# Holding the dense products of an RWKV-7 stage together on the tensor engine

## The chip, the core and the metric

The kernel runs on one core of a Trainium2 chip. The core has a tensor engine (PE, whose weight loads the profile lists as PEld), a vector engine (DVE), a scalar engine (ACT), a general engine (POOL) and a queue that issues transfers (SP). Each engine takes its instructions in the order in which the program lists them. The metric is the device time of one execution in microseconds, lower is better.

## The reference

The computation is a small decoder trunk in float32: 256 tokens of width 2048, one RWKV-7 layer, one latent-attention layer, each followed by a squared-ReLU MLP. The change is in the RWKV layer alone. Cut to what matters there:

```python
rkv = jnp.einsum('jbtd,jde->jbte', xs[:3], w_rkv)      # three 2048x2048 projections
r, k, v = rkv[0], rkv[1], rkv[2]
decay = jnp.exp(-jnp.exp(w_log))                       # w_log from tanh(xw @ w1) @ w2
a = jax.nn.sigmoid(a0 + (xa @ a1) @ a2)
g = jax.nn.sigmoid(xg @ g1) @ g2

def step(S, inp):                                      # a recurrence over 256 tokens, per head of 64
    sa = jnp.einsum('bhvk,bhk->bhv', S, -kk_t)
    S = (S * w_t[:, :, None, :] + sa[..., None] * (kk_t * a_t)[:, :, None, :]
         + v_t[..., None] * k_t[:, :, None, :])
    return S, jnp.einsum('bhvk,bhk->bhv', S, r_t)

_, y = lax.scan(step, S0, ...)
out = (group_norm(y) + bonus) * g
return out @ w_o                                       # one more 2048x2048 projection
```

## The kernel before

**Precision.** A large product is made of three products in a rounded 32-bit type (fp32r). Each operand is split into a high part (a cast on ACT, line 172) and a low part (a subtraction on DVE, line 173). For a weight they are called `whi` and `wlo`, and one half of a loaded weight block (`raw`) is 128x1024. Both come from a pool with two buffers each, and the small weights `wsm` of a tile use the same two.

**The RWKV stage.** The 2048 channels are done in 16 tiles of 128 channels (two heads). For each tile `project_rk` makes r and k: two weights of two halves each, 8 blocks a half, 3 products a block, so 96 products of 128x256 (`rk`, lines 223 to 225). These are the dense filling. `rwkv_tile` does the rest of the tile as a long chain of small steps with a `yield` after each: the small projections `wa` (decay and a) and `pg` (gate), 6 products each; matrices within the chunk (`pm`, `ar`); a triangular inverse by doubling (`pW`, `pN`, `pW`, `pN`, `pT`, `pW`, `pN`, tiles of 32 then 64, in fp32); the recurrence over two chunks (`pu`, `psS`, `prhs`, `py`); and a group norm (`yt`). Almost every step of that chain goes from PE to ACT or DVE and back to PE.

**The loop.** Up to three tiles are under way (`LONG`), each begun 9 rounds (`STAGGER`) after the one before. A round advances each of them by one step and then takes from the dense filling: in the kernel before, 16/9 of a `yield` a round, and a `yield` stands after every second block (6 products). When the last tile has begun, the filling is the output projection of the first 12 of 16 channel blocks (`out_start`, `pos`, 288 products of 128x512), 2.5 blocks a round, each block of 3 products followed by a `yield`. After the loop `proj_tail` adds the last four channel blocks (`po`), with the rows of the gate (`grow`) made on PE.

**What sets the order.** A scheduler places each engine's instructions: the order of the text gives priorities, and among what it holds to be ready the first in priority goes first. So small products stand between any two dense products where the scheduler expects them ready. One helper of the kernel fixes an order: `together` gives its first product to the scheduler and puts the others, at high priority, right behind it:

```python
    def together(*calls):
        ins = calls[0]().ins
        with tc.issue_after(ins), tc.high_priority():
            for c_ in calls[1:]:
                c_()
```

Before the change it is used for the small products of one step only (`pm`, `pW`, `pN`, `psS`).

Beside this, `pump` puts steps of another computation (conditioning columns, DVE line 320, `raw` from `in_adat_dram`) behind each weight half, at a set rate.

Of the kernel before, what the change touches and what calls it, by code (L numbers as in the profile page):

```python
# [20 lines left out]
P = 128  # L21
D = 2048
KT = D // P
T = 256
# [9 lines left out]
STAGGER = 9  # L34
# [3 lines left out]
PACE = 2.5  # L38
# [38 lines left out]
def trunk_kernel(ctx: ExitStack, tc: tile.TileContext, a, out, dbg=None):  # L77
# [65 lines left out]
    def product(*args, **kw):  # L143
        return lambda: PE.matmul(*args, **kw)

# [242 lines left out]
    with ExitStack() as s0:  # L388
# [162 lines left out]
        with ExitStack() as s2:  # L551
# [24 lines left out]
            def project_rk(i):  # L576

                ps = banks["rk"].tile([P, 512], F32, tag="rk", name="rk")
                res = []
                for w, name in enumerate(("wr", "wk")):  # L580
                    raw = load(a[name][i])
                    o = slice(w * T, (w + 1) * T)
                    for half in range(2):
                        hi = split["hi"].tile([P, 1024], F32R, tag="whi", name="whi")
                        lo = split["lo"].tile([P, 1024], F32R, tag="wlo", name="wlo")
                        hilo(hi, lo, raw[:, half * 1024 : half * 1024 + 1024])
                        pump(rate[0])
                        for j in range(8):
                            kt = half * 8 + j
                            s = slice(j * P, (j + 1) * P)  # L590
                            mm3w(ps[:, o], hi[:, s], lo[:, s], xs_at(w, 0, kt), xs_at(w, 1, kt), kt == 0, kt == KT - 1)
                            if j % 2:
                                yield
                    res.append(tmp("rk"[w] + "S"))
                    ACT.copy(res[w], ps[:, o])  # L595
                rks[i] = res

            def rwkv_tile(i):
# [9 lines left out]
                yield  # L608
                wa = tbank("wa", "rb")
                for z, (zh, zl) in enumerate(((zw_h, zw_l), (za_h, za_l))):  # L610
                    q = slice(z * P, (z + 1) * P)
                    mm3w(wa[:, z * T : (z + 1) * T], smh[:K1, q], sml[:K1, q], zh[:K1], zl[:K1], True, True)
# [116 lines left out]
                for j in range(15):  # L729
# [4 lines left out]
                    if j == 4:  # L734
                        (smh, sml), = unit(a["wsm"][i][:, T:], T)
                        yield
                    if j == 9:
                        pg_ = tbank("pg", "rb")
                        for g in range(2):
                            s = slice(g * P, (g + 1) * P)  # L740
                            mm3w(pg_[:, :T], smh[:, s], sml[:, s], sg_h[:, g, :], sg_l[:, g, :], g == 0, g == 1)
# [145 lines left out]
            def out_start():  # L887

                for i in range(KO):
                    split_o(i)  # L890
                    yield
                for n in range(4):
                    pss = [banks[k].tile([P, 512], F32, tag=k, name="pos") for k in ("rk", "mm")]
                    for g in range(KO // 4):
                        for half, (hi, lo) in enumerate(unit(a["wo"][n, g])):
                            for j in range(2):
                                kt = g * 4 + half * 2 + j
                                s = slice(j * 512, (j + 1) * 512)
                                for t in range(2):
                                    q = slice(t * P, (t + 1) * P)  # L900
                                    mm3(pss[t], o_h[:, kt, q], o_l[:, kt, q], hi[:, s], lo[:, s], kt == 0, kt == KO - 1)
                                    yield
# [6 lines left out]
            for _ in project_rk(0):  # L909
                pass  # L910
            flying, nxt, steps = [], 0, 0
            fill, owed, pace = iter(()), 0.0, 16 / STAGGER
            while nxt < KT or flying:
                if nxt < KT and len(flying) < LONG and steps >= STAGGER * nxt:
                    for _ in fill:
                        pass
                    flying.append(rwkv_tile(nxt))
                    nxt += 1
                    if nxt < KT:
                        fill = project_rk(nxt)  # L920
                    else:
# [4 lines left out]
                        fill, pace = out_start(), PACE  # L926
                        rate[0] = RATE_T
                steps += 1
                for g_ in list(flying):
                    if next(g_, 0) == 0:  # L930
                        flying.remove(g_)

                owed += pace if flying else 48
                while owed >= 1:
                    owed -= 1
                    next(fill, 0)
            for _ in fill:
                pass
# [633 lines left out]
```

## Time and profile before

| | |
|---|---|
| median of 3 runs | 2593.98 us (2587.92 to 2596.9) |
| the profiled execution | 2599.04 us |
| its span, first to last instruction | 2597.3 us |
| RWKV stage, first `rk` product to last `pos` product | from 218.7 to 779.7 us |
| PE busy over the span | 2487.8 us (96%) |
| DVE busy over the span | 1945.7 us (75%) |

Times in the text are microseconds from the start of the span. In a row of the timeline the first number is the start, the second the time from start to end; products overlap, so the distance from one start to the next is what a product costs the engine, and the busy time is not. "[0.93 <-DVE rst L159]" says that the engine stood idle for 0.93 us, and what ended it. A row with xN stands for N entries in one go; a product in plain fp32 (not fp32r) makes two entries. "PEclk" is the clock that the tensor engine was granted, as a share of full speed.

### The profile page before, as it was taken

Reading aid. Unit: us, or ns where it says so; the run is one execution under the profiler, and the core shown is the slowest. Engines: PE = TensorE matmul, PEld = TensorE weight load, DVE = VectorE, ACT = ScalarE, POOL = GpSimd, SP = SyncE. Lnnn points to the kernel's source line nnn. Section 1 sums busy time; section 2 is a strip of 40 time slices with the busy share of each in tenths; the row PEclk is TensorE's granted clock in tenths of the full one; section 3 lists DMA queues with packets and bytes.
Section 4 is the critical chain, followed back from the end, with each engine's and each line's share of the span. In section 5 each row is a group of like instructions: output and inputs, shape, how many; then the busy total and the mean of one; then the engine's idle time right before and its main releaser. Section 6 shows DMA issues by size and latency. Waiting matters only on the chain.

```text
span 2597.3 us, 39264 instructions
## 1 busy us (share of the span) xinstructions
PE 2487.8 (96%) x15048; PEld 2060.5 (79%) x15048; DVE 1945.7 (75%) x3823; ACT 1312.5 (51%) x2361; POOL 70.9 (3%) x150
## 2 busy tenths in 40 slices
PE   6998999999997999999999999999899999999998
PEld 3667887888776888888888878778788888888886
DVE  4787887888877788888888867776676665555555
ACT  3555675766646444444444456544544444444443
POOL 0000110111100000000000000000000000000000
PEclk8899998999998999999999999999999999999999
DMA  9755544455575688888888824657567555555553
GB/s 374 293 192 196 178 173 153 166 180 186 171 265 205 227 331 327 331 322 328 327 332 332 328 103 156 217 176 254 210 223 260 186 190 195 189 185 194 192 184 127
DMA packets 87885, 594.54 MB, mean 229 GB/s; under 512 B 10128, under 2 KB 14480, under 8 KB 16784
## 3 DMA queue, kind: packets, MB, share of 16 engines
q1 hardware_dynamic: 87696, 592.03, 63.0%
q8 instruction: 118, 1.93, 0.3%
q14 instruction: 71, 0.58, 0.1%
HBM read 589.89 MB, written 2.10 MB: 228 GB/s over the span
## 4 chain that ended last, share of the span: by engine, by line
PE 77%; DVE 8%; ACT 4%; issue 1%; DMA 1%; POOL 0%; DVEq 0%; ACTq 0%
PE pup L233 17%; PE pd L218 9%; PE pd L220 9%; PE pd L219 9%; PE pup L234 9%; DVE wlo L173 2%; DVE raw L320 1%; PE po L219 1%; PE po L220 1%; PE po L218 1%; PE rk L223 1%; PE rk L224 1%; PE rk L225 1%; PE pl L218 1%; PE ar L720 1%
## 5 line engine op out<-in xcount | busy, mean ns | idle before, releaser
L172 ACT CAST whi<-raw 128x1024 fp32r<-128x1024 f32 x729 | 743.9, 1023 | 895.1 <-PE pd L220 355.9
L173 DVE TENSOR_TENSOR wlo<-raw,whi 128x1024 fp32r<-128x1024 f32 x729 | 864.0, 1188 | 439.0 <-ACT whi L172 436.1
L233 PE MATMUL pup<-h,whi 128*128 128x512 f32 x1920 | 677.8, 398 | 0.0
L234 PE MATMUL pup<-h,wlo 128*128 128x256 f32 x1920 | 539.2, 281 | 0.0
L233 PEld LDWEIGHTS pup<-h,whi 128*128 128x128 f32 x1920 | 360.6, 188 | 88.5
L218 PE MATMUL pd<-whi,uh 128*128 128x512 f32 x1024 | 399.0, 390 | 0.0
L220 PE MATMUL pd<-whi,ul 128*128 128x512 f32 x1024 | 398.6, 389 | 0.0
L320 DVE SCALAR_TENSOR_TENSOR raw<-raw,crow 128x1024 f32<-128x1024 f32 x320 | 389.4, 1225 | 12.0 <-DMA raw<-in_adat_dram 12.0
L219 PE MATMUL pd<-wlo,uh 128*128 128x512 f32 x1024 | 398.4, 389 | 0.0
L234 PEld LDWEIGHTS pup<-h,wlo 128*128 128x128 f32 x1920 | 362.7, 189 | 0.5
L220 PEld LDWEIGHTS pd<-whi,ul 128*128 128x128 f32 x1024 | 192.2, 188 | 40.4
L218 PEld LDWEIGHTS pd<-whi,uh 128*128 128x128 f32 x1024 | 192.2, 188 | 40.0
L219 PEld LDWEIGHTS pd<-wlo,uh 128*128 128x128 f32 x1024 | 192.2, 188 | 39.5
L223 PE MATMUL rk<-xs,whi 128*128 128x256 f32 x512 | 155.5, 304 | 2.9 <-ACT rS L595 2.2
L225 PE MATMUL rk<-xs,wlo 128*128 128x256 f32 x512 | 150.1, 293 | 2.1 <-DVE wlo L173 2.0
L224 PE MATMUL rk<-xs,whi 128*128 128x256 f32 x512 | 148.6, 290 | 0.0
L223 PEld LDWEIGHTS rk<-xs,whi 128*128 128x128 f32 x512 | 98.7, 193 | 9.3 <-ACT rS L595 4.1
L225 PEld LDWEIGHTS rk<-xs,wlo 128*128 128x128 f32 x512 | 98.8, 193 | 4.5 <-DVE wlo L173 3.0
L224 PEld LDWEIGHTS rk<-xs,whi 128*128 128x128 f32 x512 | 98.7, 193 | 1.8
L732 DVE TENSOR_TENSOR xt<-ar,X 128x60 f32<-128x60 f32 (+14 forms) x240 | 49.3, 206 | 22.3 <-ACT ar L721 20.0
L1188 DVE TENSOR_TENSOR ya<-pd,ya 128x512 f32<-128x512 f32 x96 | 61.5, 682 | 0.0
L219 PE MATMUL pv<-wlo,xsv 128*128 128x512 f32 x128 | 55.1, 431 | 5.0 <-DVE wlo L173 4.8
(431 smaller groups left out, 3620.5 us busy)
## 6 DMA issues: line engine op xcount, KB each, us to landing
raw<-in_adat_dram SPq DMA_DIRECT2D x160, 1024.0 KB, 6.9
raw<-in_up_dram SPq DMA_DIRECT2D x128, 1024.0 KB, 4.9
raw<-in_dn_dram SPq DMA_DIRECT2D x128, 1024.0 KB, 4.9
early<-in_ada_dram SPq DMA_DIRECT2D x17, 1024.0 KB, 11.9
raw<-in_wr_dram SPq DMA_DIRECT2D x16, 1024.0 KB, 5.0
raw<-in_wk_dram SPq DMA_DIRECT2D x16, 1024.0 KB, 5.9
raw<-in_wo_dram SPq DMA_DIRECT2D x16, 1024.0 KB, 5.2
raw<-in_mo_dram SPq DMA_DIRECT2D x16, 1024.0 KB, 5.3
```

The source lines that it names most:

```text
L172: ACT.copy(hi, x)
L173: return DVE.tensor_sub(lo, x, hi.bitcast(F32))
L218: PE.matmul(ps, lh, rh, start=start, stop=False)
L219: PE.matmul(ps, lh, rl, start=False, stop=False)
L220: PE.matmul(ps, ll, rh, start=False, stop=stop)
L223: PE.matmul(ps, wh, xh, start=start, stop=False)
L224: PE.matmul(ps, wh, xl, start=False, stop=False)
L225: PE.matmul(ps, wl, xh, start=False, stop=stop)
L233: PE.matmul(ps, hi[:, s], x2[:, kt].rearrange("p e t -> p (e t)"), start=(kt == 0), stop=False)
L234: PE.matmul(ps[:, T:], lo[:, s], x2[:, kt, 0, :], start=False, stop=(kt == KT - 1))
L320: DVE.scalar_tensor_tensor(raw[:, s], raw[:, s], 1.0, crow[:, s], ALU.mult, ALU.mult, accum_out=part[:, kt, half : half + 1])
L1188: DVE.tensor_add(y, pss[t], y)
```

## The change

- A helper `products3` returns the three products of a block as calls that are not yet made, low weight part first (`wl·xh`, `wh·xh`, `wh·xl`; before, `wh·xh`, `wh·xl`, `wl·xh`).
- `project_rk` yields one run of 24 products for each weight half, `out_start` one of 12.
- The loop keeps one run in hand (`pend`): the split of the next weight half is written as soon as a run has been issued. `dense` issues a run by `together`, so that nothing comes between its products.
- The steps of `rwkv_tile` that make `wa` and `pg` yield their six products, and the loop puts them behind the run of the same round (or together by themselves in a round without one). `pg` comes at the step j == 4, where before it came one step later.
- The pace is the same, counted in products: 96/9 and 7.5 a round. A round issues runs until what is owed is used up, and so may go ahead by part of a run.

```diff
+    def products3(ps, wh, wl, xh, xl, start, stop):
+
+        return [product(ps, wl, xh, start=start, stop=False), product(ps, wh, xh, start=False, stop=False),
+                product(ps, wh, xl, start=False, stop=stop)]
...
                         pump(rate[0])
+                        run = []
                         for j in range(8):
                             kt = half * 8 + j
                             s = slice(j * P, (j + 1) * P)
-                            mm3w(ps[:, o], hi[:, s], lo[:, s], xs_at(w, 0, kt), xs_at(w, 1, kt), kt == 0, kt == KT - 1)
-                            if j % 2:
-                                yield
+                            run += products3(ps[:, o], hi[:, s], lo[:, s], xs_at(w, 0, kt), xs_at(w, 1, kt), kt == 0, kt == KT - 1)
+                        yield run, 24
...
                 (smh, sml), = unit(a["wsm"][i][:, :T], T)
-                yield
                 wa = tbank("wa", "rb")
-                for z, (zh, zl) in enumerate(((zw_h, zw_l), (za_h, za_l))):
-                    q = slice(z * P, (z + 1) * P)
-                    mm3w(wa[:, z * T : (z + 1) * T], smh[:K1, q], sml[:K1, q], zh[:K1], zl[:K1], True, True)
+                yield [p_ for z, (zh, zl) in enumerate(((zw_h, zw_l), (za_h, za_l)))
+                       for p_ in products3(wa[:, z * T : (z + 1) * T], smh[:K1, z * P : (z + 1) * P],
+                                           sml[:K1, z * P : (z + 1) * P], zh[:K1], zl[:K1], True, True)]
...
                     if j == 4:
                         (smh, sml), = unit(a["wsm"][i][:, T:], T)
-                        yield
+                        pg_ = tbank("pg", "rb")
+                        yield [p_ for g in range(2)
+                               for p_ in products3(pg_[:, :T], smh[:, g * P : (g + 1) * P], sml[:, g * P : (g + 1) * P],
+                                                   sg_h[:, g, :], sg_l[:, g, :], g == 0, g == 1)]
                     if j == 9:
-                        pg_ = tbank("pg", "rb")
-                        for g in range(2):
-                            s = slice(g * P, (g + 1) * P)
-                            mm3w(pg_[:, :T], smh[:, s], sml[:, s], sg_h[:, g, :], sg_l[:, g, :], g == 0, g == 1)
...
                         for half, (hi, lo) in enumerate(unit(a["wo"][n, g])):
+                            run = []
                             for j in range(2):
...
-                                    mm3(pss[t], o_h[:, kt, q], o_l[:, kt, q], hi[:, s], lo[:, s], kt == 0, kt == KO - 1)
-                                    yield
+                                    xh, xl = o_h[:, kt, q], o_l[:, kt, q]
+                                    run += [product(pss[t], xh, lo[:, s], start=(kt == 0), stop=False),
+                                            product(pss[t], xh, hi[:, s], start=False, stop=False),
+                                            product(pss[t], xl, hi[:, s], start=False, stop=(kt == KO - 1))]
+                            yield run, 12
...
+            def dense(more=()):
+
+                run, cost = pend[0] or ([], 0)
+                if run or more:
+                    together(*run, *more)
+                pend[0] = next(fill, None)
+                return cost
...
-            fill, owed, pace = iter(()), 0.0, 16 / STAGGER
+            owed, pace = 0.0, 96 / STAGGER
...
-                owed += pace if flying else 48
-                while owed >= 1:
-                    owed -= 1
-                    next(fill, 0)
+                owed += pace
+                if owed <= 0 or not pend[0]:
+                    owed = min(owed, 0.0)
+                    if more:
+                        together(*more)
+                while owed > 0 and pend[0]:
+                    owed -= dense(more)
+                    more = []
```

What this does to the order on PE is shown at three places. The line numbers of the changed kernel are a few higher (L806 becomes L809, L880 L883), and products that go through `together` all bear the line 144.

The first place is the inverse of tile 5 (the sixth): `pW` of 32x32, `pN`, `pT`, `pW` of 64x64. In the kernel before:

```order
L144 MATMUL pW<-T_4780,MB 32x32 x8
L880 MATMUL yt<-ident,tha 128x128 x2
L881 MATMUL yt<-rb,kc 128x256
L144 MATMUL pN<-Tt_1991,T_4780 32x32 x8
L223 MATMUL rk<-xs,whi 128x256
L224 MATMUL rk<-xs,whi 128x256
L225 MATMUL rk<-xs,wlo 128x256
L223 MATMUL rk<-xs,whi 128x256
L800 MATMUL pT<-ident,Tt_1991 64x64 x4
L224 MATMUL rk<-xs,whi 128x256
L225 MATMUL rk<-xs,wlo 128x256
L806 MATMUL pW<-T_4915,MB 64x64 x4
```

The same tile in the changed kernel:

```order
L693 MATMUL tr<-ident,bt 128x128
L694 MATMUL tr<-ident,kt 128x128
L144 MATMUL pm<-AR,kt 128x256 x4
L144 MATMUL pW<-T_4791,MB 32x32 x8
L144 MATMUL pN<-Tt_1991,T_4791 32x32 x8
L803 MATMUL pT<-ident,Tt_1991 64x64 x4
L809 MATMUL pW<-T_4935,MB 64x64 x4
L724 MATMUL ar<-Z,kc 128x384 x2
L883 MATMUL yt<-ident,tha 128x128
```

Where a few dense products, or those of another tile's `yt`, stood between the links of the chain, the links now follow each other directly. In the PE order before, this stretch from `pW` (32x32) to `pT` holds no fp32r product in one tile of 16, tile 4; in the changed order in eight (0, 1, 3, 5, 7, 9, 10 and 12).

The second place is the beginning of the recurrence, where a run had been cut after two products. Before:

```order
L851 MATMUL py<-U,MB 128x64
L223 MATMUL rk<-xs,whi 128x256
L224 MATMUL rk<-xs,whi 128x256
L144 MATMUL psS<-U,bk 64x64 x2
L144 MATMUL psS<-V,bk 64x64 x2
L852 MATMUL py<-V,MK 128x64
```

Now (`pu`, then `psS` at once, and no dense product between):

```order
L835 MATMUL pu<-rh,Tt_1991 128x64 x2
L144 MATMUL psS<-U,bk 64x64 x2
L144 MATMUL psS<-V,bk 64x64 x2
L854 MATMUL py<-U,MB 128x64
L855 MATMUL py<-V,MK 128x64
```

In the whole stage the fp32r products (`rk`, `pos`, `wa`, `pg`) stand in 207 unbroken stretches before and in 108 now. 117 and 60 of them are followed by products that use part of the array's rows or columns (`pW`, `pN`, `pT`, `pm`, `psS`).

The third place is the end of the chain of the last tile. Before, dense products stand before and behind its `yt`:

```order
L218 MATMUL pos<-whi,oh 128x512
L219 MATMUL pos<-wlo,oh 128x512
L880 MATMUL yt<-ident,tha 128x128 x2
L881 MATMUL yt<-rb,kc 128x256
L220 MATMUL pos<-whi,ol 128x512
```

Now all 288 `pos` products stand ahead of it, and nothing independent lies between `py` and `yt`:

```order
L144 MATMUL pos<-whi,ol 128x512
L835 MATMUL pu<-rh,Tt_1987 128x64 x2
L866 MATMUL tr<-ident,V 128x128 x2
L854 MATMUL py<-U,MB 128x64
L855 MATMUL py<-V,MK 128x64
L854 MATMUL py<-U,MB 128x64
L855 MATMUL py<-V,MK 128x64
L883 MATMUL yt<-ident,tha 128x128 x2
L884 MATMUL yt<-rb,kc 128x256
L354 MATMUL grow<-ident,gc 128x128 x16
L223 MATMUL po_9730<-whi,oh 128x512
```

More of the change, by code (lines that the diff above doesn't have):

```diff
@@ L890, in out_start @@
                     split_o(i)
-                    yield
+                    yield [], 3
                 for n in range(4):
@@ L900, in out_start @@
                                     q = slice(t * P, (t + 1) * P)
-                                    mm3(pss[t], o_h[:, kt, q], o_l[:, kt, q], hi[:, s], lo[:, s], kt == 0, kt == KO - 1)
-                                    yield
+                                    xh, xl = o_h[:, kt, q], o_l[:, kt, q]
[3 more added lines that the diff above has]
+                            yield run, 12
                     for t in range(2):
@@ L907, in split_o, with begin @@
                 hilo(v3(o_h[:, i, :]), v3(o_l[:, i, :]), oT[:, :, i * P : (i + 1) * P])
-            for _ in project_rk(0):
-                pass
+            fill, pend = iter(()), [None]
+            def begin(steps_):
+                nonlocal fill
+                fill = steps_
+                pend[0] = next(fill, None)
[3 more added lines that the diff above has]
+                    together(*run, *more)
+                pend[0] = next(fill, None)
+                return cost
+            begin(project_rk(0))
+            while pend[0]:
+                dense()
             flying, nxt, steps = [], 0, 0
-            fill, owed, pace = iter(()), 0.0, 16 / STAGGER
+            owed, pace = 0.0, 96 / STAGGER
             while nxt < KT or flying:
                 if nxt < KT and len(flying) < LONG and steps >= STAGGER * nxt:
-                    for _ in fill:
-                        pass
+                    while pend[0]:
+                        dense()
                     flying.append(rwkv_tile(nxt))
@@ L919, in trunk_kernel @@
                     if nxt < KT:
-                        fill = project_rk(nxt)
+                        begin(project_rk(nxt))
                     else:
@@ L925, in trunk_kernel @@
                             "p (t k) c -> p t (k c)", t=2)
-                        fill, pace = out_start(), PACE
+                        begin(out_start())
+                        pace = 3 * PACE
                         rate[0] = RATE_T
                 steps += 1
+                more = []
                 for g_ in list(flying):
-                    if next(g_, 0) == 0:
+                    r_ = next(g_, 0)
+                    if r_ == 0:
                         flying.remove(g_)
-                owed += pace if flying else 48
-                while owed >= 1:
-                    owed -= 1
-                    next(fill, 0)
-            for _ in fill:
-                pass
+                    else:
+                        more += r_ or []
+                owed += pace
[5 more added lines that the diff above has]
+                    owed -= dense(more)
+                    more = []
+            while pend[0]:
+                dense()
             for i in range(KO, KT):
```

## The prediction

> **What bounds the kernel now.** I read the page first, then busy times by stretch, then the timeline of PE in the RWKV stage. The page:
>
> ```profile
> span 2597.3 us, 39264 instructions
> PE 2487.8 (96%) x15048; PEld 2060.5 (79%) x15048; DVE 1945.7 (75%) x3823; ACT 1312.5 (51%) x2361; POOL 70.9 (3%) x150
> ```
>
> PE sets the time over the whole. The change touches only the RWKV stage; the stretches of its steady part (235 to 670) and of its end (670 to 780) read, with PE first and the granted clock after POOL:
>
> ```profile
> 235.00:670.00 435.00, 404.82 (x4257) 350.59 (x4256) 375.17 (x1246) 297.98 (x812) 60.48 (x101) 0.98 0.50 175
> 670.00:780.00 110.00, 107.22 (x755) 82.75 (x754) 85.27 (x221) 58.60 (x128) 4.61 (x8) 1.00 0.64 230
> ```
>
> PE is busy for 93% of the steady part, DVE for 86%. So there is little idle time to win, and DVE would allow at best 375 us where 435 are spent. What one product costs is seen where it stands between others:
>
> ```profile
> 505.52 0.28 PE L224 MATMUL rk<-xs,whi 128*128 128x256 f32 x1
> 505.64 0.28 PE L225 MATMUL rk<-xs,wlo 128*128 128x256 f32 x1
> 505.76 0.55 PE L825 MATMUL prhs<-V,MK 128*128 128x64 f32 x4
> ...
> 506.57 0.36 PE L223 MATMUL rk<-xs,whi 128*128 128x256 f32 x1
> 506.77 0.28 PE L224 MATMUL rk<-xs,whi 128*128 128x256 f32 x1
> 506.89 0.28 PE L225 MATMUL rk<-xs,wlo 128*128 128x256 f32 x1
> ...
> 499.97 0.28 PE L224 MATMUL rk<-xs,whi 128*128 128x256 f32 x1
> 500.18 0.34 PE L144 MATMUL psS<-U,bk 128*64 128x64 f32 x4
> ```
>
> Within a stretch a dense product starts every 0.12 us. The second of a stretch comes 0.20 us after the first (506.57 to 506.77): a stretch costs 0.08 us more than its products. What follows it starts after 0.12 us if it uses the whole array (505.64 to 505.76), and after 0.21 us if it uses part of it (499.97 to 500.18): 0.09 us more.
>
> **The cuts (removed).** The orders hold 207 stretches before and 108 after, 99 fewer, and 57 fewer are followed by a product on part of the array (117 and 60). 99 x 0.08 + 57 x 0.09 = 7.9 + 5.1 = 13.0 us less on PE. It lies on the path, as PE does. Bounds: 13 us, or nothing where PE then waits for DVE.
>
> **The cover of the chain (moved).** Each link of the inverse and of the recurrence goes PE, ACT, PE. Before, the scheduler put some dense product between most of them. The links that have nothing between show the price, above all `pN` to `pu`, which stands uncovered in 15 of 16 tiles (grouped rows, 270 to 670; idle time behind the bar):
>
> ```profile
> L832 PE MATMUL pu<-rh,Tt 128*128 128x64 f32 x104 | 16.2, 279 | 6.3 <-ACT Tt L813 6.3
> L806 PE MATMUL pW<-T,MB 64*64 64x64 f32 x104 | 9.2, 231 | 2.8 <-ACT T L802 2.8
> ```
>
> 104 entries are 26 steps `pu`, 13 of them the uncovered kind: 6.3 / 13 = 0.48 us each. In the orders I counted the links `pW`-`pN`-`pW`-`pN`-`pT`-`pW` and `pN`-`pu`-`psS` that have nothing at all between them: 20 before, 47 after (`pN`-`pu` falls from 15 to 5, `pu`-`psS` rises from 0 to 11, `pN`-`pT` from 1 to 11). 27 x 0.48 = +13.0 us. Bounds: nothing, if the waits lie where PE would have to wait for a split anyway, and about three times that, if ACT has a cast of a weight half (1023 ns in the row below) ahead of each.
>
> ```profile
> L172 ACT CAST whi<-raw 128x1024 fp32r<-128x1024 f32 x729 | 743.9, 1023 | 895.1 <-PE pd L220 355.9
> ```
>
> I take the price of the bare links. So the two effects on PE's queue cancel, and the sign rests on what the uncovered links do to the clock.
>
> **The clock.** Once in the steady part PE was granted half speed; by stretch (the clock after POOL):
>
> ```profile
> 392.10:395.50 3.40, 1.61 (x69) 1.34 (x69) 3.09 (x15) 3.31 (x11) 1.40 (x3) 1.00 0.92 364
> 395.50:416.00 20.50, 18.76 (x111) 15.32 (x112) 11.46 (x36) 10.56 (x30) 0.00 (x0) 0.50 0.39 140
> 416.00:420.00 4.00, 4.00 (x36) 4.00 (x36) 2.48 (x10) 1.78 (x4) 0.10 (x1) 1.00 0.13 33
> ```
>
> and the timeline ahead of it:
>
> ```profile
> 390.86 1.13 PE L144 MATMUL pm<-AR,kt 64*128 64x256 f32 x8
> 392.93 0.44 PE L144 MATMUL pW<-Tn,A 32*32 32x16 f32 x32 [0.93 <-DVE rst L159]
> 393.30 0.39 PE L223 MATMUL rk<-xs,whi 128*128 128x256 f32 x1
> ...
> 394.09 0.45 PE L144 MATMUL pN<-T,W 32*32 32x32 f32 x32
> 395.63 0.66 PE L880 MATMUL yt<-ident,tha 128*128 128x128 f32 x2 [1.09 <-DVE tha L876]
> ```
>
> The 3.4 us ahead of the drop hold 1.61 us of PE work, half of it on pieces of 32x32, between waits of 0.93 and 1.09 us. No single wait is long; it is a few microseconds with little on the array. The clock then stays at 0.50 for 20.5 us, since at half speed only nearly unbroken dense work fills a few microseconds. This is tile 4, the one tile of 16 in whose inverse no fp32r product stands from `pW` (32x32) to `pT`. What it cost is read from one row per tile, the `pW` of 64x64:
>
> ```profile
> 368.39 0.68 PE L806 MATMUL pW<-T,MB 64*64 64x64 f32 x8
> 400.63 1.11 PE L806 MATMUL pW<-T,MB 64*64 64x64 f32 x8 [0.46 <-ACT T L802]
> 435.98 0.68 PE L806 MATMUL pW<-T,MB 64*64 64x64 f32 x8
> 464.27 0.68 PE L806 MATMUL pW<-T,MB 64*64 64x64 f32 x8 [0.27 <-ACT T L802]
> 670.68 0.67 PE L806 MATMUL pW<-T,MB 64*64 64x64 f32 x8
> ```
>
> From 464.27 (tile 6) to 670.68 (tile 13) lie 7 steps of 29.5 us each. The step of the slow clock, 400.63 to 435.98, is 35.4 us, so the drop cost 5.9 us. The change makes eight tiles of this kind. I take it that half of them drop the clock (a choice between none and all, since each is but some 3 us long and a run of 24 may stand close by): four drops for one, three more, 3 x 5.9 = +18 us. Bounds: no drop at all (-6) and one in each of the eight (+41).
>
> [...]
>
> **The order within a block, and the splits.** A run begins with its low part, so it can't start before DVE's subtraction, where before two of three products needed only the cast. What the waits for it cost before, over the whole stage:
>
> ```profile
> L225 PE MATMUL rk<-xs,wlo 128*128 128x256 f32 x512 | 150.1, 293 | 2.1 <-DVE wlo L173 2.0
> L173 DVE TENSOR_TENSOR wlo<-raw,whi 128x1024 fp32r<-128x1024 f32 x729 | 864.0, 1188 | 439.0 <-ACT whi L172 436.1
> ```
>
> 2.0 us. The split of the next half is now written one run ahead, which hides the 1.19 us of the subtraction as long as a buffer is free; the two buffers are shared with the small weights, and a run holds its own for its whole length. Bounds: -2 us, and 64 runs x 1.19 = 76 us if each split were late. I take 0, by the row of 2.0. Behind a run that waits stand the links of all three tiles, and ACT and DVE wait for those. The small projections are made in the round of their split, where before a round lay between; they stay 12 products a tile, and I cost the move at 0 with the same row. Transfers stay as many.
>
> **The end of the stage.** Runs of 12 `pos` now stand between the links of the last tile, and none is left behind `yt`. Before, dense products covered the wait from `py` to `yt`:
>
> ```profile
> 741.68 0.42 DVE L858 TENSOR_REDUCE mean<-py 128x4 f32<-128x256 f32 x1
> ...
> 747.73 1.22 DVE L173 TENSOR_TENSOR wlo<-raw,whi 128x1024 fp32r<-128x1024 f32 x1
> 748.87 0.42 DVE L876 TENSOR_TENSOR tha<-tha,rsy 128x256 f32<-128x256 f32 x1
> ```
>
> and PE at the start of `po`:
>
> ```profile
> 783.11 0.73 PE L218 MATMUL po<-whi,oh 128*128 128x512 f32 x2 [1.62 <-ACT whi L172]
> ```
>
> From mean to the last factor DVE takes 7.6 us here, 3.7 of them for two splits and one conditioning step in between (3 passes of 1.22); about 4 us remain and are uncovered now. Against that the links of the last tile are fully covered: 110 - 107.2 = 2.8 us of idle time is what can be won. Then `po` waits for a cast, as before (1.62 us). Net +1 us; bounds -3 and +10, the latter if the weights of `po` come late.
>
> **The sum.** -13 +13 +18 +0 +1 = +19 us in the steady part and the end. Some of it can hide where PE would have waited for DVE anyway, and I take 16: 2599 + 16 = 2615 us for a profiled execution. The profiled execution of before, 2599.04, lies 5.1 us above the median, so 2610 us.
>
> **Rivals.** (A) Forecast: the clock falls in some four tiles; 2610 us. (B) Faster: the cuts go and the waits do not come, since each run leaves about 2.9 us (24 x 0.12) in which the ACT links of all tiles are done; -13 from the cuts, -6 from the drop in tile 4 that is gone: 2575 us. For it: 65 of the 112 links counted still have something between. Against it: the order on PE is fixed, and 47 links have nothing between. (C) Balance: cuts and waits cancel and the clock falls as seldom as before; 2594 us. [...] (D) The clock falls in all eight tiles, or each late split holds up all three chains: +41 and some of the waits, 2640 us. For it: a fall lasts long once it has come (20.5 us). Against it: runs of 24 give the unbroken stretch that brings the clock back. That the runs are not held can't be: the order shows 59 runs of 24 whole, and one of 120.
>
> **Numbers.** A 0.45, B 0.22, C 0.20, D 0.13. A change of 0.3%, 7.8 us, is about what can be told from none. Faster 0.22 (B), the same 0.20 (C), slower 0.58 (A and D). The range holds A and C, part of B's spread (2560 to 2585) and the nearer part of D: 2577 to 2638; A alone would have 2602 to 2625.
>
> **What would show it.** The cuts: the timeline has starts 0.12 us apart over 24 products. The waits: idle time before `psS`, `pN` and `pT` with ACT as releaser, about 13 us more in all. The clock: stretches of 0.50 in the RWKV stage, some four, each behind a tile without dense products in its inverse; its mean in the stage falls from 0.98 to about 0.94. The end: 4 us of idle PE before the last `yt`, released by DVE. The prediction is wrong if the clock keeps 1.00 through the stage, or if PE waits for DVE's splits (`rk` released by `wlo`) for more than a few microseconds.

## The result, and the profile after

The changed kernel takes 2676.57 us (median of four runs, 2669.56 to 2680.77), the kernel before beside it 2595.44: a ratio of 1.0315, with a 95% interval of 1.0284 to 1.0346. The forecast was 16 us slower; it is 81 us slower. The profiled execution, from the page:

```profile
span 2674.8 us, 39248 instructions
PE 2527.3 (94%) x15048; PEld 2095.9 (78%) x15048; DVE 1958.9 (73%) x3823; ACT 1309.5 (49%) x2361; POOL 62.8 (2%) x150
```

The span grew by 77.5 us, PE's busy time by only 39.5 of them (2527.3 against 2487.8), with the same 15048 entries. Where this lies is read from busy times by stretch, cut at the first `rk`, the last `rk` and the first `po` of each kernel. In such a row stand the bounds, the length, the busy time of PE, PEld, DVE, ACT and POOL with their entries, then PE's granted clock, the transfer share and GB/s. Before:

```profile
218.70:670.10 451.40, 419.32 (x4357) 364.46 (x4356) 382.94 (x1257) 302.74 (x819) 60.58 (x101) 0.97 0.50 176
670.10:783.10 113.00, 108.61 (x765) 83.95 (x763) 85.29 (x222) 60.98 (x132) 4.51 (x8) 1.00 0.65 235
```

After:

```profile
219.80:726.60 506.80, 445.67 (x4246) 389.21 (x4246) 389.61 (x1243) 295.26 (x803) 49.76 (x99) 0.89 0.44 155
726.60:855.80 129.20, 117.72 (x877) 92.11 (x875) 92.95 (x238) 68.26 (x151) 7.25 (x9) 0.93 0.61 216
```

The steady part is 55.4 us longer: PE is busy for 26.4 us more and idle for 29.0 us more (61.1 against 32.1). The end is 16.2 us longer, 9.1 busy and 7.1 idle. That makes 71.6 us, 35.5 busy and 36.1 idle; the other 6 lie before the first `rk` (1.1) and behind the first `po`. The last `rk` does not stand at the same place of the chain in every order: here the small products of one tile's inverse have moved behind it (4246 entries in the steady part, 4357 before). So what follows about busy time is taken over both parts together.

The busy time can be taken apart. At half clock the products of a run start 0.22 us apart (289.62 to 289.84 below) in place of 0.12. The trace's record of the clock has 129.7 us at half clock in the two parts, 23.9 before. Of the 106 us more at most half, 53 us, is lost work. Busy time rose by 35.5 only, so up to 17 us of PE work went away, and the 13 of the cuts fit in that. With those 13 the clock costs about 48 us; this is an estimate.

PE's waits from 225 to 665 (engine and line, releaser; us in all, times, longest). After:

```profile
PE pN L144 <- ACT T L790: 7.8, 7, 1.7
PE pT L803 <- ACT Tt L797: 5.0, 10, 0.9
PE psS L144 <- ACT U L837: 5.0, 9, 0.9
PE pW L144 <- DVE T L782: 4.1, 6, 1.8
PE pW L809 <- ACT T L805: 3.8, 7, 0.8
PE pm L144 <- DVE X L737: 3.5, 1, 3.5
PE rk L144 <- DVE wlo L178: 3.3, 3, 1.7
...
PE pu L835 <- ACT Tt L816: 3.0, 5, 1.0
PE wa L144 <- DVE wlo L178: 2.7, 3, 1.1
```

They are the links that the forecast named: `pN`, `pT` and `psS` instead of `pu`. Summed in the trace by the product that ends the wait, the idle time ahead of the listed links rose from 12.8 us in 31 waits to 34.9 us in 54 in the steady part. That is 23 waits more, near the 27 forecast, at 0.96 us each and not 0.48. The run waits for its low part 3.3 us in all and `wa` 2.7 (before 2.0 and 1.2), so late splits on PE are a small part. A wait for `pN` lasts 7.8 / 7 = 1.1 us in the mean: three last 0.35 or 0.36 us and four 1.65 to 1.73, and ahead of three of these four ACT makes a cast of a weight half (1.04 or 1.05 us). What happens there can be seen at one place. PE's timeline:

```profile
289.62 0.41 PE L144 MATMUL rk<-xs,whi 128*128 128x256 f32 x1
289.84 0.41 PE L144 MATMUL rk<-xs,wlo 128*128 128x256 f32 x1
...
290.90 0.44 PE L144 MATMUL pW<-T,MB 32*32 32x32 f32 x16
291.69 0.72 PE L144 MATMUL pN<-Tt,T 32*32 32x32 f32 x16 [0.36 <-ACT T L790]
293.33 0.41 PE L803 MATMUL pT<-ident,Tt 64*64 64x64 f32 x4 [0.92 <-ACT Tt L797]
294.53 1.11 PE L809 MATMUL pW<-T,MB 64*64 64x64 f32 x8 [0.79 <-ACT T L805]
...
300.00 1.12 PE L835 MATMUL pu<-rh,Tt 128*128 128x64 f32 x4 [0.45 <-ACT Tt L816]
301.47 0.48 PE L144 MATMUL psS<-U,bk 128*64 128x64 f32 x4 [0.35 <-ACT U L837]
```

ACT at the same time:

```profile
291.38 0.54 ACT L790 COPY T<-pW 32x128 f32<-32x128 f32 x2 [1.76 <-PE pW L144]
291.95 1.05 ACT L177 CAST whi<-raw 128x1024 fp32r<-128x1024 f32 x1
293.02 0.53 ACT L797 COPY Tt<-pN 32x128 f32<-32x128 f32 x2
```

and the clock:

```profile
287.00:290.40 3.40, 3.40 (x18) 0.50 0.99 364
290.40:293.80 3.40, 2.03 (x41) 1.00 0.80 275
293.80:307.50 13.70, 12.16 (x57) 0.50 0.42 155
```

(This last view holds PE alone: length, busy time, clock.) A run ends at 290.9. It frees a buffer of `whi`, and the cast of the next half (1.05 us) begins between two links, so `pT` waits 0.92 us. Up to `psS` no dense product stands between the links. The clock had been at half up to 290.4. The next 3.4 us hold 2.03 us of PE work, most of it on pieces of 32x32, and then the clock is at half again for 13.7 us, in which the links themselves take longer (`pW` 1.11 us, against 0.68 in the rows of before).

In the clock's record of the trace there are 19 stretches at half clock in the steady part and two in the end, in lengths of 3.4, 6.8, 10.2 and 13.7 us; before there were two, of 3.4 and 20.5 us.

### The profile page after: what moved, and what is told of

The parts are those of the page before. It is cut to its first block, busy times and chain, and to the rows that moved or that the text cites. A ratio compares the mean times of both kernels' runs of the same rounds, so it can differ in the third digit from the quotient of the medians.

```text
span 2674.8 us, 39248 instructions
## 1 busy us (share of the span) xinstructions
PE 2527.3 (94%) x15048; PEld 2095.9 (78%) x15048; DVE 1958.9 (73%) x3823; ACT 1309.5 (49%) x2361; POOL 62.8 (2%) x150
## 4 chain that ended last, share of the span: by engine, by line
PE 63%; DVE 2%; ACT 1%; issue 1%; DMA 0%; DVEq 0%; ACTq 0%
PE pup L238 17%; PE pd L225 9%; PE pd L223 9%; PE pd L224 9%; PE pup L239 9%; PE pl L223 1%; PE po L223 1%; PE po L224 1%; PE po L225 1%; PE pl L225 1%; PE pl L224 1%; PE psc L1460 1%; PE pkq L228 1%; PE psc L1459 1%; PE pkq L229 1%
## 5 line engine op out<-in xcount | busy, mean ns | idle before, releaser
L224 PEld LDWEIGHTS pd<-wlo,uh 128*128 128x128 f32 x1024 | 192.3, 188 | 39.5
L144 PE MATMUL rk<-xs,whi 128*128 128x256 f32 x1024 | 200.7, 297 | 0.0
L144 PEld LDWEIGHTS rk<-xs,whi 128*128 128x128 f32 x1024 | 172.5, 207 | 1.2 <-issue 1.2
L144 PE MATMUL rk<-xs,wlo 128*128 128x256 f32 x512 | 160.6, 314 | 5.9 <-DVE wlo L178 3.6
L144 PEld LDWEIGHTS rk<-xs,wlo 128*128 128x128 f32 x512 | 106.2, 207 | 11.8 <-ACT rS L600 3.5
L223 PE MATMUL pv<-whi,xsv 128*128 128x512 f32 x128 | 52.6, 425 | 1.6 <-ACT whi L177 1.6
L225 PE MATMUL pv<-whi,xsv 128*128 128x512 f32 x128 | 53.9, 421 | 0.0
```

The lines of the kernel that those rows point to most:

```text
L223: PE.matmul(ps, lh, rh, start=start, stop=False)
L224: PE.matmul(ps, lh, rl, start=False, stop=False)
L225: PE.matmul(ps, ll, rh, start=False, stop=stop)
```

## Experiments

All times are ratios to the kernel before, run beside each kernel. Three theories: **K**, stretches with little on the array halve the clock, and that is a cause; **W**, the held run makes the links of all tiles wait, and the clock only follows; **S**, late splits, the low part first, or projections made in the round of their split. Later ones bear **G** (size of the doses) and **P** (place of the projections).

| kernel | ratio [95%] | first to last `rk`: us, PE busy, PE idle, clock | last `rk` to first `po`: us, clock | at half clock in both: us |
|---|---|---|---|---|
| before | 1 | 451.4, 419.3, 32.1, 0.97 | 113.0, 1.00 | 23.9 |
| after | 1.0315 [1.0284, 1.0346] | 506.8, 445.7, 61.1, 0.89 | 129.2, 0.93 | 129.7 |
| e1 | 1.0141 [1.0097, 1.0185] | 478.3, 435.4, 42.9, 0.95 | 119.5, 0.96 | 61.4 |
| e2 | 1.0154 [1.0125, 1.0182] | 459.1, 420.8, 38.3, 0.96 | 127.0, 0.95 | 47.8 |
| e3 | 1.0279 [1.0251, 1.0308] | 492.7, 434.6, 58.1, 0.92 | 128.5, 0.93 | 99.9 |
| e4 | 1.0183 [1.0155, 1.0212] | 475.6, 425.5, 50.1, 0.93 | 129.8, 0.95 | 78.6 |
| e5 | 1.0479 [1.0462, 1.0496] | 534.4, 458.1, 76.3, 0.85 | 152.1, 0.87 | 198.0 |
| e6 | 1.0439 [1.0422, 1.0456] | 523.3, 465.9, 57.4, 0.89 | 149.1, 0.93 | 140.0 |
| e7 | 1.0123 [1.0100, 1.0145] | 466.5, 428.1, 38.4, 0.95 | 125.5, 0.92 | 71.7 |
| e8 | 1.0112 [1.0094, 1.0129] | 472.5, 440.6, 31.9, 0.92 | 124.5, 0.93 | 95.6 |
| e9 | 1.0136 [1.0110, 1.0162] | 466.3, 433.7, 32.6, 0.93 | 132.1, 0.87 | 99.0 |
| e10 | 1.0054 [1.0034, 1.0074] | 455.5, 417.2, 38.3, 0.98 | 116.2, 0.97 | 27.3 |
| e11 | 1.0042 [1.0025, 1.0060] | 465.2, 428.9, 36.3, 0.96 | 110.3, 1.00 | 41.0 |
| e12 | 1.0322 [1.0298, 1.0346] | 506.9, 443.8, 63.1, 0.89 | 134.1, 0.87 | 143.3 |
| e13 | 1.0068 [1.0043, 1.0093] | 472.9, 436.2, 36.7, 0.95 | 107.9, 1.00 | 44.4 |
| e14 | 1.0093 [1.0070, 1.0115] | 465.5, 424.9, 40.6, 0.97 | 109.3, 1.00 | 23.9 |
| e15 | 1.0140 [1.0110, 1.0169] | 467.4, 425.5, 41.9, 0.97 | 117.1, 0.97 | 34.1 |

The right columns are those of the stretches as above, from one profiled execution each; a median may lie some us from it. As the last `rk` moves along the chain from order to order, the two parts of different kernels are best compared by their sum. 0.1% is 2.6 us.

### Undoing the held runs: e1, e2, e7, e12

e1 gives the dense products to the scheduler one by one; all else is as in the changed kernel.

```diff
-                if run or more:
-                    together(*run, *more)
+                for c_ in run:
+                    c_()
+                if more:
+                    together(*more)
```

> The changed kernel, with the dense products given to the scheduler one by one instead of as a held run (the small projections of a round are still held together, the order within a block, the split one run ahead and the early gate projection stay). In its PE order no tile is without dense products in its inverse, 13 links are bare (47 in the changed kernel, 20 before), and there are 155 stretches. Theory K (stretches with little on the array pull the clock to half): 2590 to 2610 us, under 40 us at half clock in the RWKV stage (130 in the changed kernel). Theory S (late splits, the low part first, projections made in the round of their split): stays at 2655 or more, with PE waits on wlo. Theory W (a held run makes the links of all three tiles wait, the clock is a by-product): also near 2600.

e2 holds only the output products; e7 holds nothing; in both the small projections are as before the change.

```diff
-                if run or more:
-                    together(*run, *more)
+                if cost == 12:          # e7: without this branch
+                    together(*run)
+                else:
+                    for c_ in run:
+                        c_()
```

> Only the output projection is held in runs of 12; r and k products go one by one, and the small projections are made as before, one round after their split. 5 bare links, 161 stretches. Theories K and W: 2575 to 2600 us, the end of the stage (last rk product to first po product) near the 112 us of before; if runs of 12 are what harms the end, it is near the 129 us of the changed kernel. Theory S expects about 2600 too, since the projections are back where they were, so here it is the end that is read.

> Nothing is held: r, k and output products go one by one, and the small projections are made as before. What is left of the change is the low part first in a block and the split one run ahead. Against the run with only the output held (2633, 127 us at the end of the stage, 459 steady): the end falls back to 113 to 119 us and the steady part stays at 455 to 462, so 2605 to 2622 us. If the end stays at 127, runs of 12 are not its cause.

e12 is the changed kernel with the output products alone given one by one (`if cost == 12`, each by itself).

> The changed kernel with one part undone: the output products of the last stretch are placed one by one and not in runs of 12. Theory W (the runs of 12 make the end of the stage 16 us longer): 2660 to 2668 us, with the stretch from the last r/k product to the first po at 113 to 118 us in place of 129. Theory K (the end of the stage is longer because the last links come later and at half clock, whatever is held there): 2670 to 2680 us, the stretch 124 us or more.

Measured: e1 1.0141, e2 1.0154, e7 1.0123, e12 1.0322. Not holding the runs wins back 1.7% (43 us; 1.0315 against 1.0141), the largest single part. The idle time ahead of the links is back at 13.3 us in 31 waits, as before the change. Even so e1, with 2633 us, lies outside the ranges of all three theories, and it has 61 us at half clock where K had under 40; `wa` waits 7.1 us for its low part in the steady part (1.2 before), so S has a small part. From e1 to the changed kernel the two parts grow by 38.2 us, 23.8 idle and 14.4 busy, while the time at half clock doubles: W's waits and K's clock are both in the price of holding.

e2 missed its 2575 to 2600 us by 33. The runs of 12 of the output cost nothing that shows: e12 is as slow as the changed kernel, and its end is no shorter (134.1 against 129.2 us). e2 and e7 differ by 8 us, within their intervals. So W fell for the end of the stage, and K's expectation for e12 held. And e7 was the surprise: with nothing held and the projections as before, 1.2% (32 us) are still lost, 4 us more than the range allowed, and its end stays at 125.5 us.

### The length of a run: e4, e15, e3

e4 has runs of 12 in r and k, e15 of 6; all else as changed.

```diff
-                        yield run, 24
+                            if len(run) == 12:      # e15: 6
+                                yield run, 12
+                                run = []
```

> The r and k runs are 12 products long instead of 24, all else as in the changed kernel. 32 bare links, 2 tiles without dense products in the inverse, 135 stretches. Theory K: between, 2615 to 2650 us, 50 to 90 us at half clock in the stage. Theory W: half the hold-up, about 2640. Theory S: stays at 2665 or more.

> The changed kernel with runs of 6 in r and k, all else as in it (projections in the round of their split and joined to a run, output in runs of 12). Theory G: between e14 and e4_runs_of_12 (2642 us), 2612 to 2630 us: the loss grows with the length of the run. Theory K without G (what counts is that projections stand in the inverse): no better than e8_before_joined and e9, 2622 to 2640 us.

e3 keeps the runs of 24 and makes `wa` and `pg` as before the change: a `yield` between split and products, one by one, `pg` at j == 9.

> Runs of 24 and 12 held as in the changed kernel, but wa and pg are made as before, one round after their split and not joined to a run. 53 bare links, 14 tiles without dense products in their inverse. Theory K: as slow as the changed kernel or slower, 2670 to 2710, over 130 us at half clock in the stage. Theory S (projections made too early are what holds up PE): back to 2600 to 2630. Theory W: about 2676, as the runs are the same.

Measured: 6, 12 and 24 products give 1.0140, 1.0183 and 1.0315. In the table PE's idle time goes 41.9, 50.1, 61.1 us, the clock 0.97, 0.93, 0.89 and the time at half clock 34, 79, 130 us. The idle time ahead of the links of the chain is 20.9, 21.3 and 34.9 us (37, 37 and 54 waits). e4 lies in K's range and at W's value, and e15 in the ranges of both G and K, so the times of these two separate none of them.

ACT's waits for a half of the weight to come free grow too, from 225 to 665. Runs of 6:

```profile
ACT whi L177 <- PE rk L144: 12.6, 16, 2.3
```

Runs of 12:

```profile
ACT whi L177 <- PE rk L144: 33.0, 25, 5.1
```

Runs of 24:

```profile
ACT whi L177 <- PE rk L144: 53.0, 23, 5.3
```

But these waits are not what the loss goes by. The kernel before has

```profile
ACT whi L172 <- PE rk L224: 36.3, 26, 5.3
```

and e1, with no run held in r and k, 43 us faster than the changed kernel,

```profile
ACT whi L177 <- PE rk L144: 58.6, 31, 4.7
```

while e3, with runs of 24, has

```profile
ACT whi L177 <- PE rk L144: 24.4, 15, 5.4
```

What a cast costs when it falls into a bare link is seen in the rows at 291.95 above. That longer runs make the casts fall there more often is not shown.

e3, 1.0279, lies 0.36% under the changed kernel, with intervals that overlap. It is nearest to W's value (2676); K had 2670 or more with over 130 us at half clock, and it is 2664 with 100; S had 2630 at most. Holding the runs alone, of 24 and 12 (e7 to e3), costs 1.56%, 40 us.

### Is the clock a cause? e5 and e6

To fill the links with work needs a place for its results. e5 is the control: the changed kernel with one bank fewer for `rt`. e6 puts three products that nobody reads (`fl`, 128x256) behind `pW`, `pN`, `pT` and the first `pu` of each tile, 192 in all. To do so it also holds `pT` and `pu` together, which e5 does not.

```diff
-            psum(s2, rk=1, mm=2, py=1, rt=2, rb=2)
+            psum(s2, rk=1, mm=2, py=1, rt=1, rb=2)      # e6: and fl=1
...
+                return [product(FL[:, :T], w_, x_, start=True, stop=True) for _ in range(n)]
...
-                            for m_ in range(4) for p_, e, o in halves))
+                            for m_ in range(4) for p_, e, o in halves), *filler())
```

> The changed kernel with one PSUM bank instead of two for the inverse's tiles (this frees a bank; it is the control for the next run). All theories: within 15 us of the changed kernel, 2665 to 2690 us, with 100 to 140 us at half clock in the RWKV stage.

> The control, with three dense products whose result nobody reads (128x256, into the freed bank) put right behind each of four links of a tile's chain, the two pW and pN of 32x32 and pT of the inverse and the first pu: 192 products, 64 x (3 x 0.12 + 0.17 for the cuts) = 34 us of added PE work, of which some 15 us fall into waits that PE has anyway. Theory K (the half clock is a cause): the time at half clock in the stage falls below 60 us and the kernel gets faster than its control by 10 to 30 us although it does more. Theory W (the clock only follows the waits, which come from held runs): slower than the control by 10 to 30 us.

e5 missed its expectation: the bank costs 1.6%, and the time at half clock is 198 us, not 100 to 140. e6 is faster than its control (1.0439 against 1.0479, intervals apart) though it does more. From the stretches, e5:

```profile
216.60:751.00 534.40, 458.09 (x4178) 399.06 (x4178) 389.21 (x1201) 292.00 (x789) 51.95 (x96) 0.85 0.41 146
```

and e6:

```profile
221.60:744.90 523.30, 465.92 (x4330) 407.66 (x4331) 390.04 (x1200) 292.67 (x789) 51.40 (x96) 0.89 0.42 148
```

At 0.12 us each, 192 products are 23 us of work. Most of it went into idle time (57.4 against 76.3 us), and PE's busy time rose by 8 us only, since the clock was higher (0.89 against 0.85). The kernel with this work is 12 us faster, as K had it (10 to 30), and W's sign was wrong. But the time at half clock fell from 198 to 140 us, not below 60 as K had it. The order on PE is not the same in the two either: some 150 of 5120 entries stand elsewhere, `pu` of several tiles behind a run instead of ahead of it. So this pair speaks for K, and does not show that the filling alone did it. That the clock costs time where PE does not wait longer is shown by e8 and e9.

### The small projections: e8, e9, e10, e13

Four edits of the kernel before. e8 makes `wa` and `pg` in the round of their split and holds the six together; e9 only makes them in that round; e10 only holds them, in their old round. In e8 and e10 their low parts also come first.

```diff
                 (smh, sml), = unit(a["wsm"][i][:, :T], T)
-                yield                                     # e8, e9
...
-                    mm3w(wa[:, z * T : (z + 1) * T], ...)  # e8, e10: the six by together
+                yield                                     # e8, e9
```

> The kernel before, with nothing changed but the small projections: made in the round of their split and held together, as in the change; dense products as before. Theory S for this part (they wait for a split that is not ready, with all three chains behind them): 2608 to 2622 us, with PE waits of wa and pg on wlo of 5 to 12 us. If the join costs something only beside held runs: 2590 to 2602.

> The kernel before with one change: the small projections (wa, pg) are made in the round of their split, one by one and not held together. Theory K (the loss of the joined projections, +29 us, is clock: six small products that stand together among the 32x32 pieces leave the array nearly empty): no run of six stands there, the clock falls about as seldom as before, 2590 to 2605 us. Theory S (being made in the round of their split, they and what is behind them wait for the split): the loss stays, 2612 to 2625 us, with several us more idle PE before wa and pg released by wlo.

> The kernel before with one change: the six products of wa, and those of pg, are held together, in the round in which they were before. Theory K: the same drops of the clock as with joined and moved projections, 2608 to 2625 us, the time at half clock in the RWKV stage rises from 24 us to 60 or more. Theory S: a round lies between split and products again, so no loss, 2590 to 2602 us.

Measured: 1.0112, 1.0136 and 1.0054. The move by one round is what costs, with nothing held, 1.4% or 35 us: the expectation of K for e9 (2590 to 2605 us) was wrong, and e10 lost 14 us, between both expectations, without the drops that K wanted (27 us at half clock). S was nearer in time (e8 1 us, e9 6 us above its ranges), but wrong on the reason. e9 in the steady part and the end:

```profile
220.00:686.30 466.30, 433.68 (x4254) 373.52 (x4253) 379.51 (x1241) 298.51 (x807) 57.66 (x99) 0.93 0.49 169
686.30:818.40 132.10, 126.32 (x869) 97.47 (x867) 90.01 (x239) 65.33 (x144) 5.88 (x9) 0.87 0.58 207
```

Together they are 34.0 us longer than before, with as many entries (5123, 5122 before): PE is busy for 32.1 us more and idle for 1.9 more. The time at half clock is 75 us longer, which allows up to 37 us of lost work. In e8 it is 32.6 us, 30.3 busy and 2.3 idle. PE waited for `wa`'s split 1.8 us in e9 and 1.2 before. Here is one place in e9:

```profile
463.69 0.44 PE L144 MATMUL pW<-T,MB 32*32 32x32 f32 x16 [0.72 <-DVE T L779]
...
464.75 0.72 PE L144 MATMUL pN<-Tt,T 32*32 32x32 f32 x16
465.86 0.39 PE L223 MATMUL wa<-zwh,whi 97*128 97x256 f32 x1 [0.39 <-ACT whi L172]
466.08 0.28 PE L224 MATMUL wa<-zwl,whi 97*128 97x256 f32 x1
466.29 0.41 PE L800 MATMUL pT<-ident,Tt 64*64 64x64 f32 x4
```

and its clock, around the next drop:

```profile
465.10:468.50 3.40, 3.00 (x34) 2.20 (x35) 2.05 (x5) 3.09 (x9) 0.00 (x0) 1.00 0.83 275
468.50:471.90 3.40, 3.40 (x10) 1.72 (x11) 1.79 (x6) 2.58 (x5) 0.00 (x0) 0.50 0.59 248
```

`wa` now stands in the inverse of another tile, 0.4 us ahead of its `pT`. In the kernel before, it stands 6.6 us behind it:

```profile
462.70 0.38 PE L800 MATMUL pT<-ident,Tt 64*64 64x64 f32 x4
...
469.34 0.29 PE L223 MATMUL wa<-zwh,whi 97*128 97x256 f32 x1
```

Is it that place that matters? e13 moves the split a round later instead, so that split and products share a round but the products keep their place (8.4 us behind `pT` at this tile).

```diff
-                (smh, sml), = unit(a["wsm"][i][:, :T], T)
                 yield
+                (smh, sml), = unit(a["wsm"][i][:, :T], T)
```

> The kernel before with one change: the split of the small weights is made one round later, in the round of the products wa and pg, which stay in their old round. So here split and products share a round as in e9_before_moved (+35 us), but the products keep their place among the links of the other tiles. Theory P (place: the move hurts since wa and pg then stand in the inverse of another tile): no loss, 2585 to 2602 us, the first wa 5 to 9 us behind the pT of another tile as before. Theory S (round of the split): PE waits for the split as in e9, 2612 to 2635 us.

e13 gives 1.0068, between the two expectations. About half of the loss of e9 (0.68 of 1.36%) is gone, though its profiled execution took 2618.7 us, 7 more than the median. Its steady part is longer than that of e9 (472.9 against 466.3 us), but holds 117 entries more, those of a tile that in e9 lies in the end; the two parts together are 580.8 us against 598.4, with 44 us at half clock against 99 (24 before). Between `pW` (32x32) and `pT` of some tile stand 51 of the 192 products of `wa` and `pg` in e9, and none in e13 or before. PE waits 4.6 us for the small splits up to 690, so S has a small part here. So the place explains much of the loss, and not all. That e8 and e9 lose by the clock and not by waiting is shown; which trait of the new order brings the drops that are left is open.

### The rest: e11, e14

e11 is the kernel before with the low part first in each block of r and k. e14 is e7 with doses of 6 products instead of 24, nothing held.

```diff
-                            mm3w(ps[:, o], hi[:, s], lo[:, s], xs_at(w, 0, kt), xs_at(w, 1, kt), kt == 0, kt == KT - 1)
+                            PE.matmul(ps[:, o], lo[:, s], xs_at(w, 0, kt), start=kt == 0, stop=False)
+                            PE.matmul(ps[:, o], hi[:, s], xs_at(w, 0, kt), start=False, stop=False)
+                            PE.matmul(ps[:, o], hi[:, s], xs_at(w, 1, kt), start=False, stop=kt == KT - 1)
```

> The kernel before with one change: each block of r and k begins with the low part of the weight. Theory S (late splits: what is left of the loss, about 24 us in the steady part, when nothing is held and the projections are as before): 2605 to 2620 us, with several us more of PE waiting for wlo. Theory K: PE waits little more for wlo; the time follows what the scheduler's new order does to the clock, 2594 to 2610 us.

> e7_nothing_held (nothing held, projections as before, 2626 us) with r and k handed out in doses of 6 products, not 24. Theory G (coarse doses: 24 products at one point of the program and none in the next round or two leave links uncovered): most of what e7 lost beyond the order in the block (2606 in e11_before_low) comes back, 2600 to 2612 us. Theory S (the split written ahead of its use holds a buffer and is what costs): 2620 to 2630 us.

e11: 1.0042, 11 us, where the ranges of K and S overlap; PE's wait for `wlo` went from 2.0 to 3.7 us only, and the time at half clock from 24 to 41. e14: 1.0093, 24 us, between both expectations, with no more time at half clock than before. Of the 32 us that e7 loses with nothing held, 11 go with the order in the block, if the parts add; the size of a dose makes some 8 at most, with intervals that overlap. The rest (the split written ahead, the new loop) was not tried alone.

## Why the prediction was wrong

The direction was right, by the reason given (the uncovered links cost, and then the clock). The size was five times too small. By its steps:

- **What bounds the kernel**: held. PE is the bound, and it is busy for 88% of the steady part (93% before).
- **The cuts**: -13 us fits in the 17 at most that the busy time leaves for them. It was not measured alone.
- **The cover of the chain**: +13 us forecast, and the listed links wait 22 us longer in the steady part and 2 in the end. Their number was right (23 waits more, 27 forecast). Their price failed: 0.96 us and not 0.48. The upper bound ("three times that", with a cast on ACT ahead of each link) had the cause of the longest. Idle time that the sum does not have comes to it: about 7 us net in the steady part, ahead of `wa`, the first `pW` and `pm`.
- **The clock**: this is the step that failed most. "Half of eight tiles" gave four drops, three more of 20.5 us each, and +18 us. There were 21 instead of two, 106 us more at half clock and not 61, at a price of about 48 us in the two parts. The price of a drop was read too low as well. The drop of before begins at 395.5, and 5.1 us of it lie ahead of the row at 400.63, in a step of 32.2 us: the two steps from 368.39 to 435.98 are 8.6 us longer than two of 29.5 (their own waits included), not 5.9. The reason given for the drop's length fits both traces: in the last 3.41 us of each of the 23 drops (two before, 21 after) PE is busy for 3.34 us or more, though in five of them an earlier 3.41 us was as full and the clock stayed at half. And the count of tiles without dense products in the inverse was no guide. In the order of e3 there are 14 such tiles, in that of the changed kernel eight, and e3 has the higher clock (0.92 against 0.89); e1 has none and is at half clock for 61 us. Drops come at `pu` and `psS` and behind small projections as well (at 512.28 and at 502.04 in the changed kernel).
- **The order within a block, and the splits**: 0 was taken, since PE waited 2.0 us for `wlo`. It waits 3.3 us now, so that reading held. But the edits costed by that row were not free: low part first 11 us (e11), moved projections 35 us in the kernel before (e9), some 9 in the changed one (e3, within the intervals). For the move the row could not show it, since the loss of e9 is in the clock and not in a wait.
- **The end of the stage**: +1 us forecast, +16.2 measured, some 4 us of it (an estimate from its rows) a tile's inverse that has moved there. The wait named came, 4.6 us ahead of the last `yt` (waits from 727 to 857):

```profile
PE yt L883 <- DVE tha L879: 5.0, 2, 4.6
PE po L223 <- ACT whi L177: 3.1, 1, 3.1
```

but not what was to pay for it: idle time rose from 4.4 to 11.5 us, and the clock fell there too. e12, with loose output products, has 0.6 us of this `yt` wait and an end just as long at a clock of 0.87. What sets the length of the end is open.
- **Rivals**: B and C fell. D (2640 us) was nearest. Of its two causes the clock went further than its eight tiles, and of late splits PE's own waits show only 4 us more (`rk` and `wa`, steady part). Long waits do not mark the drops: one of the 21 comes at the end of a wait of 3.52 us and one 1.4 us into the wait of 4.62 us; ahead of the other 19 no wait is longer than 1.8 us.

By edits, and if the parts add, the 81 us are: about 32 that are there with nothing held (e7, of them 11 for the low part first), about 40 for holding the runs (e7 to e3; 43 from e1), and up to 9 for the projections. Holding the output costs nothing that shows.

## What to carry to other kernels

When a tensor engine serves a long chain of small steps, the dense work between the links can be worth more than the breaks it suffers. Here a break costs 0.17 us at most, a bare link 0.35 to 1.7 us, the longest where another engine does a piece of other work (a cast of 1.05 us) ahead of the link's own step, and behind a few microseconds with little on the array the clock was at half for 3.4 to 13.7 us (the changed kernel's drops). Wherever an edit moves work by a round, do not cost it at nothing because no wait shows: e9 lost 35 us so, with PE idle for 1.9 us more. Look at what will stand next to it on PE.

## What was not expected of the hardware

The clock fell while PE was busy: 3.00 of 3.40 us ahead of the drop at 468.5 in e9 above, and all of 3.40 us ahead of one in e5, on `pW` and `pN` of 32x32 and on `pm`:

```profile
396.00:399.40 3.40, 3.40 (x72) 2.12 (x72) 3.37 (x8) 2.20 (x8) 3.12 (x2) 1.00 0.02 5
399.40:413.10 13.70, 9.99 (x69) 7.98 (x70) 8.39 (x25) 6.75 (x19) 1.82 (x4) 0.50 0.45 151
```

So PE's busy share does not settle what the clock does. For an estimate each entry of a product is weighted by the part of the 128x128 array that it uses and by its columns (at 0.12 us for 256), and summed over each window of 3.41 us (the shortest stretch in the clock's record) at full clock, from the first `rk` to the first `po`, over all 17 profiled executions. 203 windows were followed by a drop, 2391 were not. All 203 have a weighted share of 0.43 or less; from 0.45 on there is no drop in 1859 windows. Below 0.2, 102 of 107 are followed by one, and between 0.2 and 0.3 it is 63 of 184. How the two entries of a plain fp32 product count is not known: at half weight each it is 122 of 272 below 0.2, and still none from 0.45 on. So in these runs drops came only with little on the array. That this is what the clock goes by is not shown.

And filling may pay: with products that nobody reads a kernel was 12 us faster (e6 against e5), though its order had changed as well.
